# RWKV outputs in one run per group of four chunks, and half-array matmuls that alternate between two heads

## The chip, the cores and the metric

The kernel runs on one core of a Trainium2 chip. A core has a matrix engine (TensorE, PE in the profile) that multiplies a stationary operand, loaded beforehand, by a moving one and writes to PSUM, eight banks of accumulators; a vector engine (VectorE, DVE), a scalar engine (ScalarE, ACT), a general engine (GpSimd, POOL), and queues that start DMA transfers (SyncE, SP). The engines work side by side, each in its own order, and wait for each other through semaphores. The metric is the device time of one execution in microseconds (us), median of several runs; lower is better.

## The reference

One decoder layer over 2048 tokens of width 1024, in fp32: a mixer of two groups of heads, a cross-attention to 256 memory tokens, a SwiGLU feed-forward network, each with a norm ahead and a residual add. The change touches the mixer alone, and in it mainly the eight RWKV heads of width 64:

```python
def rwkv7_scan(r, w, k, v, a, b):
    def step(S, inp):
        r_t, w_t, k_t, v_t, a_t, b_t = inp
        sa = jnp.einsum('bhij,bhj->bhi', S, a_t)
        S = S * w_t[:, :, None, :] + sa[..., None] * b_t[:, :, None, :] + v_t[..., None] * k_t[:, :, None, :]
        return S, jnp.einsum('bhij,bhj->bhi', S, r_t)
```

Each head keeps a 64x64 state S that is updated at every token; the token's output is the new state times r. The outputs are then normalised per head, gated, and multiplied with the output weights together with the outputs of four mLSTM heads.

## The kernel before

The stages follow each other: a pass that transposes the normed input, the mixer, the output projection, attention, and the feed-forward network in two parts. `mixer` calls `mixer_pass` four times; a pass handles two RWKV heads and one mLSTM head for all tokens. Tokens go in super-groups of 256, eight to a pass; a super-group is four chunks of 64 tokens. The two RWKV heads of a pass lie in the two halves of the 128 partitions (`halves`: 0 to 63 and 64 to 127).

A pass takes two super-groups at a time:

- `prepare` (L295) projects k, r and v with f16 matmuls that use the whole array (three products of high and low parts, `mm3`, L52 to L55), derives the decays with the low-rank products `wps` (L317), and forms per chunk the operands of the scan. `AR` holds side by side a (64 columns) and r (64 columns), scaled by decays; `KB` the two kinds of keys. The products of `KB` and `AR` (`aps`, L379) are made per head on that head's 64 rows, four chunks of 128 columns to a PSUM bank; DVE masks them into `M`, `RA` and `AY` (L381, L382, L384), and ACT copies a part of `AR` into `RA` (L383). `KB` is transposed on PE (`kbps`, L390) and copied to `KBt` (L391).
- `solve` (L394) inverts the strict triangles `M` of the chunks: POOL does it for blocks of 32, with DMAs to bring them into rows, and PE joins the blocks with 32x32 matmuls (`pps`, L438, and `xps`, L443), first all of one head and then all of the other, with an ACT copy after each.
- `scan` (L446) walks through the four chunks one after another. For each chunk, three matmuls per head follow each other, with a copy between: `RA` times `VS` (L457, copy L459), `M` times that (L466, copy L469 into `VX`), `KBt` times `VX` (L471), from which DVE makes the next chunk's state (L475). `VS` holds the state in one half of its rows and v in the other. Then come the outputs y of the chunk: `AR`'s r part, on the head's 64 rows, times the state (L478), and `AY` times `VX` (L479) on all 128, into `yps`; after every second chunk DVE copies `yps` to `y` (L481). `tail` normalises and gates y later.
- the mLSTM head's work on the same tokens (`mlstm`) follows, again mostly full-array f16 matmuls.

The order in which instructions stand on each engine is not that of the source. A planner simulates the program on a model of the engines and places each instruction when its operands would be ready, with the source order as its priority. So PE's queue holds the scan's short steps with f16 matmuls of the projections between them. Tiles come from pools with a number of buffers; who writes a buffer again waits for its last reader. The pool `sl` (five buffers to a name) holds what a super-group hands from `prepare` to `scan`, `t1` has one buffer to a name. The PSUM pool `pax`, two banks, serves `wps`, `sps`, `bps`, `vps`, `aps` and `kbps` in turn; `psc` has one bank for `ch`, the scan's steps, and one for `yps`.

Of the kernel before, what the change touches and what calls it, by code (L numbers as in the profile page):

```python
# [165 lines left out]
def pre_pass(c, I, T, pool):  # L166
    """u^T = normed x, the RWKV low-rank activations and the mLSTM gate rows, for all tokens."""
# [77 lines left out]
def mixer_pass(c, I, hp, tp, T):  # L245
    """The RWKV heads 2*hp and 2*hp + 1 and the mLSTM head hp; leaves y^T in DRAM."""
# [48 lines left out]
    def prepare(sg, u, M):  # L295
# [6 lines left out]
        g.AR = sl.tile([P, 4, P], F32, tag="AR", name="AR")  # L302
        g.RA = sl.tile([P, 4, 2, 64], F32, tag="RA", name="RA")
# [47 lines left out]
        nc.vector.scalar_tensor_tensor(g.AR[:, :, 0:64], sq.rearrange(v4, n=4), c.kk[:, 0, ct:ct + 1], E[:, :, 0:64],  # L351
# [9 lines left out]
        nc.vector.tensor_tensor(g.AR[:, :, 64:128], r.rearrange(v4, n=4), E[:, :, 1:65], ALU.mult)  # L361
# [10 lines left out]
        for h in range(2):  # L372
            nc.gpsimd.tensor_copy(g.VX[halves[1 - h], :, h], g.VS[halves[1 - h], :, h])
        for h in range(2):
            b, ob = halves[h], halves[1 - h]
            kc = slice(64 * (1 - h), 64 * (1 - h) + P)
            aps = tp.pax.tile([P, 4, P], F32, tag="ax", name="aps")
            for n in range(4):
                nc.tensor.matmul(aps[:, n], lhsT=KB[b, n, kc], rhs=g.AR[b, n], start=True, stop=True)  # L379
            bc = lambda r, cc: c.mask[r, cc].unsqueeze(1).to_broadcast([r.stop - r.start, 4, 64])  # L380
            nc.vector.tensor_tensor(g.M[b], aps[b, :, 0:64], bc(b, b0), ALU.mult)  # L381
            nc.vector.tensor_tensor(g.RA[ob, :, h], aps[ob, :, 0:64], bc(ob, b0), ALU.mult)  # L382
            nc.scalar.copy(g.RA[b, :, h], g.AR[b, :, 0:64])  # L383
            nc.vector.tensor_tensor(g.AY[:, :, h], aps[:, :, 64:128], bc(slice(0, P), b1), ALU.mult)  # L384
        for h in range(2):
            b = halves[h]
            kc = slice(64 * (1 - h), 64 * (1 - h) + P)
            kps = tp.pax.tile([P, 4, 64], F32, tag="ax", name="kbps")
            for n in range(4):
                nc.tensor.transpose(kps[:, n], KB[b, n, kc], c.ident[b, b])  # L390
            nc.scalar.copy(g.KBt[:, :, h], kps)  # L391
        return g

    def solve(MX, NG):  # L394
        """Turns each chunk's strict triangle M into the transposed inverse of I - M^T, in place."""
# [39 lines left out]
        lohi = [(slice(64 * h, 64 * h + 32), slice(64 * h + 32, 64 * h + 64)) for h in range(2)]  # L435
        for a, b in lohi:
            for i in range(NU):
                nc.tensor.matmul(pps[b, i], lhsT=MXu[a, i, 32:64], rhs=T1[a, i], start=True, stop=True)  # L438
            nc.scalar.copy(T1[b].rearrange("p n (c e) -> p n e c", e=2), pps[b].rearrange("p n (e c) -> p n e c", e=2))
        xps = tp.psx.tile([P, NU, 32], F32, tag="sx", name="xps")  # L440
        for a, b in lohi:
            for i in range(NU):
                nc.tensor.matmul(xps[a, i], lhsT=T1[b, i], rhs=MXu[b, i, 32:64], start=True, stop=True)  # L443
            nc.scalar.copy(MXu[a, :, 32:64], xps[a])

    def scan(sg, g, g2, fresh):  # L446
# [4 lines left out]
        for n in range(4):  # L451
            ch = tp.psc.tile([P, 3, 64], F32, tag="ch", name="ch")
            if n % 2 == 0:
                yps = tp.psc.tile([P, 2, 64], F32, tag="Y", name="yps")
            to = halves[n % 2]
            for h in range(2):
                nc.tensor.matmul(ch[halves[h], 0], lhsT=g.RA[:, n, h], rhs=g.VS[:, n, h], start=True, stop=True)  # L457
# [12 lines left out]
            for h in range(2):  # L470
                nc.tensor.matmul(ch[halves[h], 2], lhsT=g.KBt[:, n, h], rhs=g.VX[:, n, h], start=True, stop=True)  # L471
# [4 lines left out]
            for h in range(2):  # L476
                b = halves[h]
                nc.tensor.matmul(yps[to, h], lhsT=g.AR[b, n, 64:128], rhs=g.VS[b, n, h], start=True, stop=False)  # L478
                nc.tensor.matmul(yps[to, h], lhsT=g.AY[:, n, h], rhs=g.VX[:, n, h], start=False, stop=True)  # L479
            if n % 2 == 1:  # L480
                nc.vector.tensor_copy(y[:, n // 2], yps)  # L481
# [168 lines left out]
def mixer(c, I, T):  # L650
    tc = c.tc
    with ExitStack() as ctx:
        tp = Ctx()
        for name, bufs, space in (("x", 2, None), ("w", 10, None), ("u", 8, None), ("t2", 1, None),
                                  ("t1", 1, None), ("m2", 2, None), ("k", 2, None), ("sl", 5, None), ("s2", 2, None), ("MX", 3, None), ("pmm", 2, PSUM),
                                  ("pax", 2, PSUM), ("psc", 1, PSUM), ("psx", 1, PSUM), ("pml", 1, PSUM)):
            kw = {"space": space} if space is not None else {"side": "right"} if name == "sl" else {}
            setattr(tp, name, ctx.enter_context(tc.tile_pool(name=f"x{name}", bufs=bufs, reuse_waits="tile", **kw)))
        for hp in range(4):
# [750 lines left out]
```

## Time and profile before

| | |
|---|---|
| median of 3 runs | 3165.73 us (3163.65 to 3174.46) |
| span of the profiled execution | 3167.2 us |
| PE, DVE, ACT, POOL busy | 97%, 68%, 41%, 38% of the span |
| mixer, about 104 to 1480 us: PE busy | 1334.8 of 1376 us |
| records of L478 and L479, the outputs | 512 each |
| records of L379 (aps), L390 (kbps) | 512, 256 |
| records of L438 (pps), L443 (xps) | 512 each |

The profile is of one execution, and the span is that execution's own time. A group of instructions is given by its line in the kernel, engine, operation, the tiles written and read, the rows x columns of the array that a matmul uses, and the number of records; an fp32 matmul leaves two records, an f16 matmul or an fp32 transpose one. In the order of time, a row gives start and length in us, and instructions of one kind that stand together are merged with their number. The length of a matmul is modelled; its start is measured.

### The profile page before, as it was taken

The page shows a single profiled execution, that of the slowest core. Times are in us where ns is not written, and L with a number is a line of the kernel's source. Part 1 is how long each engine was busy: PE and PEld are TensorE (multiplying, and loading weights), DVE is VectorE, ACT ScalarE, POOL GpSimd, SP SyncE. Part 2 cuts the span into 40 slices and gives each one's busy share as a digit, 9 for nine tenths or more (in the row PEclk, how much of TensorE's full clock was granted, in tenths as well). Part 3 has the DMA queues.
Part 4 walks back from the last instruction along what each step waited for, and adds up shares of the span by engine and source line. Part 5 has one row for each costly group of instructions (what it writes and reads, how often), then busy time and mean ns, then how long its engine had stood idle before and what let it go on. Part 6 is the DMA issues. An engine that isn't in the chain of part 4 may idle for free. (4 is left out here: it accounts for less than half of the span.)

```text
span 3167.2 us, 55759 instructions
## 1 busy us (share of the span) xinstructions
PE 3065.2 (97%) x20515; PEld 1855.3 (59%) x20515; DVE 2162.1 (68%) x4182; ACT 1290.2 (41%) x3098; POOL 1190.6 (38%) x2179
## 2 busy tenths in 40 slices
PE   7899999999999999999999999999999999899998
PEld 4688777777777767755645554444444444344444
DVE  6567877676767757744878888555554444897975
ACT  6444544454445434522756664222222222423432
POOL 2165545454545446201511124222222221553642
PEclk9899999899999989899999999999999999999999
DMA  8522422232213222554423337212112111454442
GB/s 271 128 75 60 106 61 74 60 96 61 72 47 81 71 72 67 162 167 154 144 84 120 115 129 281 81 54 67 56 58 74 54 53 54 165 188 157 133 145 83
DMA packets 393966, 331.01 MB, mean 105 GB/s; under 512 B 92654, under 2 KB 343772, under 8 KB 392796
## 3 DMA queue, kind: packets, MB, share of 16 engines
q1 hardware_dynamic: 393692, 327.45, 34.3%
q8 instruction: 161, 2.64, 0.4%
q14 instruction: 113, 0.93, 0.1%
HBM read 231.86 MB, written 95.49 MB: 103 GB/s over the span
## 5 line engine op out<-in xcount | busy, mean ns | idle before, releaser
L53 PE MATMUL pp<-u,wb 128*128 128x512 f16 x1232 | 468.1, 380 | 12.3 <-DVE e L1115 8.4
L54 PE MATMUL pp<-u,wb 128*128 128x512 f16 x1232 | 467.9, 380 | 0.0
L55 PE MATMUL pp<-u,wb 128*128 128x512 f16 x1232 | 467.6, 380 | 0.0
L1115 DVE TENSOR_TENSOR e<-pp,e 128x512 f32<-128x512 f32 x308 | 208.5, 689 | 300.3 <-PE pp L55 287.5
L55 PE MATMUL dps<-w,gS 128*128 128x512 f16 x616 | 234.1, 380 | 9.2 <-DVE gS L49 9.2
L54 PE MATMUL dps<-w,gS 128*128 128x512 f16 x616 | 234.2, 380 | 1.7 <-DVE w L49 1.7
L53 PE MATMUL dps<-w,gS 128*128 128x512 f16 x616 | 234.0, 380 | 0.0
L420 POOL TENSOR_TENSOR X<-X,tmp 64x126 f32<-64x126 f32 (+22 forms) x496 | 203.6, 410 | 31.0
L54 PEld LDWEIGHTS <-wb 128*128 128x128 f16 x1232 | 120.8, 98 | 155.6 <-issue 11.8
L418 POOL TENSOR_TENSOR tmp<-M,X 64x126 f32<-64x126 f32 (+22 forms) x496 | 187.0, 377 | 61.6 <-DMA M<-md 34.4
L53 PEld LDWEIGHTS <-wb 128*128 128x128 f16 x1232 | 120.8, 98 | 150.1 <-DMA u<-u_d 4.3
L55 PEld LDWEIGHTS <-wb 128*128 128x128 f16 x1232 | 120.8, 98 | 146.3 <-issue 1.3
L1131 POOL TENSOR_TENSOR S<-raw 128x512 f32<-128x512 f32 x22 | 33.8, 1536 | 405.0 <-DVE wb L49 405.0
L53 PEld LDWEIGHTS <-wh 128*128 128x128 f16 x1280 | 128.9, 101 | 27.0 <-issue 2.5
L53 PE MATMUL qps<-uh,wh 128*128 128x256 f16 x512 | 144.3, 282 | 0.0
L54 PE MATMUL qps<-ul,wh 128*128 128x256 f16 x512 | 144.0, 281 | 0.0
L54 PEld LDWEIGHTS <-wh 128*128 128x128 f16 x1280 | 129.0, 101 | 25.4 <-issue 4.2
L55 PE MATMUL qps<-uh,wl 128*128 128x256 f16 x512 | 143.7, 281 | 0.0
L55 PEld LDWEIGHTS <-wl 128*128 128x128 f16 x1280 | 129.2, 101 | 22.9 <-issue 1.7
L53 PE MATMUL vops<-wh,uh 128*128 128x256 f16 x512 | 139.8, 273 | 0.8 <-ACT cv L533 0.6
L55 PE MATMUL vops<-wh,ul 128*128 128x256 f16 x512 | 139.8, 273 | 0.0
L54 PE MATMUL vops<-wl,uh 128*128 128x256 f16 x512 | 139.8, 273 | 0.0
(430 smaller groups left out, 8104.8 us busy)
## 6 DMA issues: line engine op xcount, KB each, us to landing
g_d<-e SPq DMA_DIRECT2D x88, 256.0 KB
uh<-u_d SPq DMA_DIRECT2D x144, 128.0 KB
ul<-u_d SPq DMA_DIRECT2D x144, 128.0 KB
h<-h_d SPq DMA_DIRECT2D x32, 512.0 KB
acc<-h_d SPq DMA_DIRECT2D x32, 512.0 KB
u_d<-ub SPq DMA_DIRECT2D x56, 256.0 KB
ga<-g_d SPq DMA_DIRECT2D x32, 384.0 KB
raw<-in_ffn_w_gate_dram SPq DMA_DIRECT2D x22, 512.0 KB
```

Source lines behind the costliest of these rows:

```text
L53: nc.tensor.matmul(out, lhsT=lhs[0], rhs=rhs[0], start=start, stop=False)
L54: nc.tensor.matmul(out, lhsT=lhs[0], rhs=rhs[1], start=False, stop=False)
L55: nc.tensor.matmul(out, lhsT=lhs[1], rhs=rhs[0], start=False, stop=stop)
L418: nc.gpsimd.tensor_tensor(tv, M[:, s, s + 1:32].unsqueeze(2).to_broadcast(shp), X[:, s, 0:ncl].unsqueeze(1).to_broadcast(shp), ALU.mult)
L420: nc.gpsimd.tensor_tensor(X[:, s + 1:32, 0:ncl], X[:, s + 1:32, 0:ncl], tv, ALU.add)
L1115: add = lambda o, x, y: nc.vector.tensor_tensor(o, x, y, ALU.add)
L1131: nc.gpsimd.tensor_tensor(s[0], a[1][0], a[1][1], ALU.add)
```

## The change

Outputs: `AR` becomes a tile with one buffer, and a new tile `RR` of five buffers, [128, 4 chunks, 2 heads, 128], takes the place of `RA`. Its first 64 columns are what `RA` held. Its last 64 hold r on the head's own rows, copied by ACT together with the other part, and zeros on the other head's rows, which POOL writes once ahead of the passes. So the product with r now runs over all 128 rows, where the v part of `VS` meets the zeros. The outputs of all four chunks are made after the scan's last matmul of the super-group (`issue_after` sets their place on PE behind it), in a `yps` of four times 64 columns, and DVE copies it once.

Alternation: the matmuls of `wps`, `aps`, `kbps`, `pps` and `xps`, which use a part of the array's rows, no longer do all of one head and then the other, but one of each in turn. For `wps`, `aps` and `kbps` both heads' banks are taken ahead. The copies after `pps` and `xps` follow when both heads are done. The diff also takes docstrings out.

```diff
-        g.AR = sl.tile([P, 4, P], F32, tag="AR", name="AR")
-        g.RA = sl.tile([P, 4, 2, 64], F32, tag="RA", name="RA")
+        AR = tp.t1.tile([P, 4, P], F32, tag="AR", name="AR")
+        g.RR = next(tp.RR)
...
-        wps = []
-        for q in range(2):
-            b = halves[q]
-            wps.append(tp.pax.tile([P, SGN], F32, tag="ax", name="wps"))
-            mm3(nc, wps[q], (c.lwa[0][b, cs], c.lwa[1][b, cs]), (xwa[0][b], xwa[1][b]), True, True)
+        wps = [tp.pax.tile([P, SGN], F32, tag="ax", name="wps") for _ in range(2)]
+        for x, y in ((0, 0), (0, 1), (1, 0)):
+            for q in range(2):
+                b = halves[q]
+                nc.tensor.matmul(wps[q], lhsT=c.lwa[x][b, cs], rhs=xwa[y][b], start=x + y == 0, stop=x == 1)
...
+        kcs = [slice(64 * (1 - h), 64 * (1 - h) + P) for h in range(2)]
+        axs = [tp.pax.tile([P, 4, P], F32, tag="ax", name="aps") for _ in range(2)]
+        for n in range(4):
+            for h in range(2):
+                b = halves[h]
+                nc.tensor.matmul(axs[h][:, n], lhsT=KB[b, n, kcs[h]], rhs=AR[b, n], start=True, stop=True)
         for h in range(2):
-            b, ob = halves[h], halves[1 - h]
-            kc = slice(64 * (1 - h), 64 * (1 - h) + P)
-            aps = tp.pax.tile([P, 4, P], F32, tag="ax", name="aps")
-            for n in range(4):
-                nc.tensor.matmul(aps[:, n], lhsT=KB[b, n, kc], rhs=g.AR[b, n], start=True, stop=True)
+            b, ob, aps = halves[h], halves[1 - h], axs[h]
...
-            nc.vector.tensor_tensor(g.RA[ob, :, h], aps[ob, :, 0:64], bc(ob, b0), ALU.mult)
-            nc.scalar.copy(g.RA[b, :, h], g.AR[b, :, 0:64])
+            nc.vector.tensor_tensor(g.RR[ob, :, h, 0:64], aps[ob, :, 0:64], bc(ob, b0), ALU.mult)
+            nc.scalar.copy(g.RR[b, :, h], AR[b])
...
+        kps = [tp.pax.tile([P, 4, 64], F32, tag="ax", name="kbps") for _ in range(2)]
+        for n in range(4):
+            for h in range(2):
+                b = halves[h]
+                nc.tensor.transpose(kps[h][:, n], KB[b, n, kcs[h]], c.ident[b, b])
         for h in range(2):
-            b = halves[h]
-            kc = slice(64 * (1 - h), 64 * (1 - h) + P)
-            kps = tp.pax.tile([P, 4, 64], F32, tag="ax", name="kbps")
-            for n in range(4):
-                nc.tensor.transpose(kps[:, n], KB[b, n, kc], c.ident[b, b])
-            nc.scalar.copy(g.KBt[:, :, h], kps)
+            nc.scalar.copy(g.KBt[:, :, h], kps[h])
...
+        for i in range(NU):
+            for a, b in lohi:
+                nc.tensor.matmul(pps[b, i], lhsT=MXu[a, i, 32:64], rhs=T1[a, i], start=True, stop=True)
         for a, b in lohi:
-            for i in range(NU):
-                nc.tensor.matmul(pps[b, i], lhsT=MXu[a, i, 32:64], rhs=T1[a, i], start=True, stop=True)
             nc.scalar.copy(T1[b].rearrange("p n (c e) -> p n e c", e=2), pps[b].rearrange("p n (e c) -> p n e c", e=2))
...
-            for h in range(2):
-                b = halves[h]
-                nc.tensor.matmul(yps[to, h], lhsT=g.AR[b, n, 64:128], rhs=g.VS[b, n, h], start=True, stop=False)
-                nc.tensor.matmul(yps[to, h], lhsT=g.AY[:, n, h], rhs=g.VX[:, n, h], start=False, stop=True)
-            if n % 2 == 1:
-                nc.vector.tensor_copy(y[:, n // 2], yps)
+        yps = tp.psc.tile([P, 2, 2, 64], F32, tag="Y", name="yps")
+        with tc.issue_after(last.ins):
+            for m in range(2):
+                for h in range(2):
+                    for n in (2 * m, 2 * m + 1):
+                        nc.tensor.matmul(yps[halves[n % 2], m, h], lhsT=g.RR[:, n, h, 64:128], rhs=g.VS[:, n, h],
+                                         start=True, stop=False)
+                    for n in (2 * m, 2 * m + 1):
+                        nc.tensor.matmul(yps[halves[n % 2], m, h], lhsT=g.AY[:, n, h], rhs=g.VX[:, n, h],
+                                         start=False, stop=True)
+        nc.vector.tensor_copy(y, yps)
...
+        rr = [tp.RR.tile([P, 4, 2, P], F32, name=f"RR{i}") for i in range(5)]
+        for t in rr:
+            tc.nc.gpsimd.memset(t[64:128, :, 0, 64:128], 0.0)
+            tc.nc.gpsimd.memset(t[0:64, :, 1, 64:128], 0.0)
+        tp.RR = cycle(rr)
```

More of the change, by code (lines that the diff above doesn't have):

```diff
@@ L350, in prepare @@
         nc.vector.tensor_tensor(sq, sq, k, ALU.mult)
-        nc.vector.scalar_tensor_tensor(g.AR[:, :, 0:64], sq.rearrange(v4, n=4), c.kk[:, 0, ct:ct + 1], E[:, :, 0:64],
+        nc.vector.scalar_tensor_tensor(AR[:, :, 0:64], sq.rearrange(v4, n=4), c.kk[:, 0, ct:ct + 1], E[:, :, 0:64],
                                        op0=ALU.mult, op1=ALU.mult)
@@ L360, in prepare @@
         nc.scalar.copy(KB[:, :, 128:192], KB[:, :, 0:64])
-        nc.vector.tensor_tensor(g.AR[:, :, 64:128], r.rearrange(v4, n=4), E[:, :, 1:65], ALU.mult)
+        nc.vector.tensor_tensor(AR[:, :, 64:128], r.rearrange(v4, n=4), E[:, :, 1:65], ALU.mult)
         nc.vector.scalar_tensor_tensor(ta, r, col(c, R_RK + ct), ta, op0=ALU.mult, op1=ALU.mult)
@@ L435, in solve @@
         lohi = [(slice(64 * h, 64 * h + 32), slice(64 * h + 32, 64 * h + 64)) for h in range(2)]
+        for i in range(NU):
+            for a, b in lohi:
+                nc.tensor.matmul(pps[b, i], lhsT=MXu[a, i, 32:64], rhs=T1[a, i], start=True, stop=True)
         for a, b in lohi:
-            for i in range(NU):
-                nc.tensor.matmul(pps[b, i], lhsT=MXu[a, i, 32:64], rhs=T1[a, i], start=True, stop=True)
             nc.scalar.copy(T1[b].rearrange("p n (c e) -> p n e c", e=2), pps[b].rearrange("p n (e c) -> p n e c", e=2))
         xps = tp.psx.tile([P, NU, 32], F32, tag="sx", name="xps")
+        for i in range(NU):
+            for a, b in lohi:
+                nc.tensor.matmul(xps[a, i], lhsT=T1[b, i], rhs=MXu[b, i, 32:64], start=True, stop=True)
         for a, b in lohi:
-            for i in range(NU):
-                nc.tensor.matmul(xps[a, i], lhsT=T1[b, i], rhs=MXu[b, i, 32:64], start=True, stop=True)
             nc.scalar.copy(MXu[a, :, 32:64], xps[a])
@@ L452, in scan @@
             ch = tp.psc.tile([P, 3, 64], F32, tag="ch", name="ch")
-            if n % 2 == 0:
-                yps = tp.psc.tile([P, 2, 64], F32, tag="Y", name="yps")
-            to = halves[n % 2]
             for h in range(2):
-                nc.tensor.matmul(ch[halves[h], 0], lhsT=g.RA[:, n, h], rhs=g.VS[:, n, h], start=True, stop=True)
+                nc.tensor.matmul(ch[halves[h], 0], lhsT=g.RR[:, n, h, 0:64], rhs=g.VS[:, n, h], start=True, stop=True)
             R = tp.s2.tile([P, 64], F32, tag="R", name="R")
@@ L470, in scan @@
             for h in range(2):
-                nc.tensor.matmul(ch[halves[h], 2], lhsT=g.KBt[:, n, h], rhs=g.VX[:, n, h], start=True, stop=True)
+                last = nc.tensor.matmul(ch[halves[h], 2], lhsT=g.KBt[:, n, h], rhs=g.VX[:, n, h], start=True, stop=True)
             for h in range(2):
@@ L654, in mixer @@
         for name, bufs, space in (("x", 2, None), ("w", 10, None), ("u", 8, None), ("t2", 1, None),
-                                  ("t1", 1, None), ("m2", 2, None), ("k", 2, None), ("sl", 5, None), ("s2", 2, None), ("MX", 3, None), ("pmm", 2, PSUM),
+                                  ("t1", 1, None), ("m2", 2, None), ("k", 2, None), ("sl", 5, None), ("RR", 1, None), ("s2", 2, None), ("MX", 3, None), ("pmm", 2, PSUM),
                                   ("pax", 2, PSUM), ("psc", 1, PSUM), ("psx", 1, PSUM), ("pml", 1, PSUM)):
-            kw = {"space": space} if space is not None else {"side": "right"} if name == "sl" else {}
+            kw = {"space": space} if space is not None else {"side": "right"} if name in ("sl", "RR") else {}
             setattr(tp, name, ctx.enter_context(tc.tile_pool(name=f"x{name}", bufs=bufs, reuse_waits="tile", **kw)))
+        rr = [tp.RR.tile([P, 4, 2, P], F32, name=f"RR{i}") for i in range(5)]
[3 more added lines that the diff above has]
+        tp.RR = cycle(rr)
         for hp in range(4):
```

## Prediction

> **What bounds the kernel now.** I read the page's totals first, then the busy time of the two halves of the span, then what PE waited for in the first half, and last the order of time on PE around the matmuls that the change touches.
>
> ```profile
> span 3167.2 us, 55759 instructions
> PE 3065.2 (97%) x20515; PEld 1855.3 (59%) x20515; DVE 2162.1 (68%) x4182; ACT 1290.2 (41%) x3098; POOL 1190.6 (38%) x2179
> ```
> ```profile
> 104.00:1480.00 1376.00, 1334.81 (x11770) 1015.87 (x11768) 933.60 (x2414) 600.69 (x1824) 612.92 (x1654) 0.96 0.32 85
> 1480.00:3167.00 1687.00, 1649.72 (x8002) 789.06 (x8000) 1164.24 (x1630) 623.39 (x1152) 555.95 (x448) 1.00 0.34 110
> ```
> ```profile
> PE ch L457 <- DVE RA L382: 4.4, 1, 4.4
> ```
>
> All edits lie in the mixer, which runs from about 104 to 1480 us (columns of the second fence: stretch, its length, then busy us of PE, weight loads, DVE, ACT, POOL; then the granted clock). PE is busy for 1335 of 1376 us there, DVE for 934, ACT 601, POOL 613. The wait that costs PE most in this stretch (third fence: total us, times, longest) comes to 4.4 us, and its whole idle time to 41. So the order of PE's own instructions sets the pace, and a microsecond taken from PE's queue counts, unless other work then ends last. A busy PE is no proof of dense PE, because a record's end is modelled; the start times say more, and the rest is built on them.
>
> **The price of a change of array shape.** The timeline gives start, length, line, tiles, rows x columns of the array, and how many records were merged; an fp32 matmul leaves two records.
>
> ```profile
> 182.81 0.27 PE L54 MATMUL rps<-ul,wh 128*128 128x256 f16 x1
> 182.92 0.27 PE L55 MATMUL rps<-uh,wl 128*128 128x256 f16 x1
> 183.12 1.71 PE L379 MATMUL aps<-AR,KB 64*128 64x128 f32 x16
> 184.76 0.28 PE L53 MATMUL vps<-uh,wh 128*128 128x256 f16 x1
> ```
> Two full-array f16 matmuls start 0.11 us apart. The step from a full one to one on 64 rows is 0.20, so each such crossing costs some 0.09 us, and the way back costs too. That is the first thing that the change can save; the second is that two parts of the array can work at once:
>
> ```profile
> 609.45 0.27 PE L479 MATMUL yps<-VX,AY 128*64 128x64 f32 x1
> 609.45 0.27 PE L471 MATMUL ch<-VX,KBt 128*64 128x64 f32 x1
> 609.55 0.22 PE L479 MATMUL yps<-VX,AY 128*64 128x64 f32 x1
> 609.56 0.33 PE L471 MATMUL ch<-VX,KBt 128*64 128x64 f32 x3
> 609.82 0.33 PE L478 MATMUL yps<-VS,AR 64*64 64x64 f32 x2
> ```
> Matmuls that write different halves of the output partitions start within 0.01 us of each other.
>
> **The outputs (y).** 512 records of each kind, two to a matmul, are 128 chunks of two heads; and one chunk in order of time, in two places:
>
> ```profile
> L478 PE MATMUL yps<-VS,AR 64*64 64x64 f32 x512 | 85.0, 247 | 2.6 <-DVE VS L475 2.5
> L479 PE MATMUL yps<-VX,AY 128*64 128x64 f32 x512 | 83.3, 245 | 4.0 <-ACT VX L469 4.0
> ```
> ```profile
> 702.26 0.46 PE L390 MATMUL kbps<-ident,KB 64*128 64x64 f32 x4
> 702.65 0.32 PE L478 MATMUL yps<-VS,AR 64*64 64x64 f32 x2
> 702.91 0.34 PE L457 MATMUL ch<-VS,RA 128*64 128x64 f32 x4
> 703.17 0.46 PE L390 MATMUL kbps<-ident,KB 64*128 64x64 f32 x4
> ...
> 709.89 0.34 PE L471 MATMUL ch<-VX,KBt 128*64 128x64 f32 x4
> 710.06 0.28 PE L479 MATMUL yps<-VX,AY 128*64 128x64 f32 x2
> 710.27 0.33 PE L478 MATMUL yps<-VS,AR 64*64 64x64 f32 x2
> 710.52 0.33 PE L479 MATMUL yps<-VX,AY 128*64 128x64 f32 x2
> 710.78 0.28 PE L54 MATMUL vops<-wl,uh 128*128 128x256 f16 x1
> ```
> The early L478 takes 702.65 to 702.91, 0.26. Later, 709.89 to 710.78 is 0.89; four records of this shape with the way out take 0.26 (L457, 702.91 to 703.17), so the y part is 0.63. Together 0.89 a chunk, 128 of them: 114 us.
>
> What comes in its place is one run a group of four chunks: 16 matmuls, all 128 rows by 64 columns, alternating between the halves of the output. In the 609 us fence six records take 0.37 to the next shape, against 0.26 for four: a matmul more in the same half costs 0.11. Eight to each half, side by side: 0.9 a group when the run joins L471, which has the same shape, and 1.2 with its own way in and out. I take 1.05; 32 groups make 34 us. If the halves didn't overlap it would be 16 x 0.11 = 1.8, or 58. Net **-80** (bounds -56 and -85).
>
> **aps (L379).**
> ```profile
> 340.26 1.16 PE L379 MATMUL aps<-AR,KB 64*128 64x128 f32 x8
> 341.35 0.28 PE L53 MATMUL qps<-uh,wh 128*128 128x256 f16 x1
> ```
> One head alone costs 1.09 and the crossing into it 0.09: 1.18, two apart 2.36. Back to back, from 183.12 to 184.76 and a crossing, they cost 1.73, less than sixteen records one after another, so the second head's first records already run beside the first head's last. Alternating all the way should come near one head's time, 1.25. In the timeline five of 32 groups stand back to back, 27 apart: 27 x 1.1 + 5 x 0.5 = **-32** (with no more overlap than none, a crossing pair saved: -8).
>
> **wps, kbps, pps and xps.**
> ```profile
> 706.15 0.28 PE L53 MATMUL wps<-xwa,lwa 64*128 64x256 f16 x1
> ...
> 706.58 0.28 PE L53 MATMUL vops<-wh,uh 128*128 128x256 f16 x1
> ```
> ```profile
> 166.66 0.29 PE L53 MATMUL wps<-xwa,lwa 64*128 64x256 f16 x2
> ...
> 167.10 0.28 PE L53 MATMUL kps<-uh,wh 128*128 128x256 f16 x1
> ```
> ```profile
> 319.43 0.47 PE L390 MATMUL kbps<-ident,KB 64*128 64x64 f32 x8
> 319.84 0.28 PE L55 MATMUL vps<-uh,wl 128*128 128x256 f16 x1
> ```
> ```profile
> 542.79 0.69 PE L438 MATMUL pps<-T,MX 32*32 32x32 f32 x16
> 543.41 0.28 PE L53 MATMUL wps<-xwa,lwa 64*128 64x256 f16 x1
> ```
> The crossing in, 0.09, is added to each. wps: one head's three cost 0.43 + 0.09 = 0.52; where both heads' stand together already, six cost 0.44 + 0.09, about as much. Some 20 groups are apart: 20 x 0.5 = **-10** (-4 for the crossings alone). kbps: four cost 0.39 + 0.09 = 0.48 (702.26 above); eight together 0.41 + 0.09 = 0.50. About 24 groups are apart: 24 x 0.46 = **-11** (-5). pps and xps: sixteen records cost 0.62 + 0.09 = 0.71; 16 solves with two products of two heads. Alternating I expect 0.76 for both: 32 x 0.66 = **-21**; without overlap only the crossings, 0.2 each, -6.
>
> The Trainium skill (TensorE: Matmul & The Clock Gate, the section "Wait — 56ns, not 53.3ns?") says that starts of matmuls never lie closer than about 25 ns. The rows at 609.45 disagree for neighbouring halves; but if it held on the average for the 32x32 records, 32 of them would need 0.8 us, and pps and xps would give -13, the sum 8 less.
>
> **What is added, and its cover.**
> ```profile
> L379 PE MATMUL aps<-AR,KB 64*128 64x128 f32 x512 | 77.2, 297 | 7.1 <-DVE Sc L475 2.4 <-DVE VS L475 2.0 <-ACT RA L383 1.4
> L383 ACT COPY RA<-AR 64x256 f32<-64x256 f32 x64 | 25.7, 402 | 4.2 <-DVE AR L351 3.5
> L384 DVE TENSOR_TENSOR AY<-aps,mask 128x256 f32<-128x256 f32 x64 | 26.6, 416 | 0.5
> L373 POOL COPY VX<-VS 64x256 f32<-64x256 f32 x64 | 28.9, 451 | 53.3 <-ACT VS L371 40.0 <-PE yps L479 8.9 <-issue 1.8
> ```
> The ACT copy into RR is twice as wide, at most 0.40 us more in each of 64: 26 us on an engine that is idle for 775 of 1376, ahead of a solve that lies between it and its use; 0 taken, 13 if it were on the chain once a group. Ten memsets on POOL, by the nearest copy 0.45 each, 4.5 us once, while POOL has nothing to do (taken as 0). The y copies on DVE become half as many and twice as wide, slightly less. AR now has one buffer, so the next prepare's writes of it wait for the aps matmuls and the two copies; both come within a few us of the write and the next write a whole prepare later: 0. The run stands ahead of the next group's L457 and can hold it up by its 1.05 us; the y matmuls between chunks hold the chain up by 0.89 a chunk today: 0, and 34 at worst. The sum on PE is **-154**; with every lower bound it is -79.
>
> **How much of it reaches the end.** The half-speed clock is the other loss of this stage:
> ```profile
> 578.60:588.80 10.20, 9.55 (x51) 6.88 (x51) 5.36 (x16) 3.21 (x12) 2.99 (x8) 0.50 0.04 6
> ```
> The mean of 0.96 over the mixer's 1376 us is worth some 50 us, and PE's idle time 41. Both come where the f16 filler runs out and PE follows the scan's chain; there the y matmuls now stand in the gaps, and taking them out leaves a wait. DVE's share rises from 68 to 74%. I let these losses grow by 40, nearly by half: -154 + 40 = -114, and 3167.2 - 114 = 3053. The median of the runs lies 1.5 below the profiled execution: **3052 us**.
>
> **Rivals.** (1) The alternation brings no more overlap than there is, only fewer crossings: -79, with losses that grow by 20, half as much: 3107. Against it speak the wps and kbps fences, where the overlap is there.
> (2) The chain takes over: waits and half-speed stretches double, +90: 3102. For it: the 0.50 row above. Against: the scan's steps have f16 work beside them nearly everywhere. The Trainium skill (the same page, "HAM oscillation — how this bites in real kernels") ties the half-speed clock to idle gaps over some 3.4 us; the row at 578.60 has PE busy for 9.55 of 10.20 us at 0.50, so here it takes less. By the page no clock would be lost to short waits, only the waits would double: 3167 - 154 + 41, the forecast's own time.
> (3) The run doesn't stay together: the planner may set f16 matmuls between its pairs, since only its beginning is tied. A pair alone costs 0.26 + 0.09 = 0.35, eight 2.8 a group, 90 in all; y then saves 24, the sum is 98, and with the same 40 lost it is 3108.
> (4) **Slower.** Both banks of the pool that aps, kbps, wps, sps, bps and vps share are now claimed together. PE's queue is in order: kbps for both heads stands behind the masks of both, six DVE operations of 0.42 (2.5 us); aps stands behind four ACT copies out of vps, the next wps behind two KBt copies, none longer than L383's 0.40 (2.4 us). That is 4.9 us a group if none is covered; with 0.6 us lost to a clock that falls in such gaps, 5.5 x 32 = 176, and 3167 - 154 + 176 = 3189, 3188 as a median. It decides only from 4.8 us uncovered a group, 44 f16 steps that the planner would have failed to put there; today PE's idle time ahead of L379 is 7.1 us over all 32 groups, so it is unlikely.
>
> **Chances.** Forecast 0.62, (1) 0.12, (2) 0.12, (3) 0.06, (4) 0.08, a quarter of which near no change. A difference under 0.3% (9.5 us) is about what can't be told from no change. Faster 0.91, within 0.03, slower 0.06. The range goes from the whole sum and 15 us of regained clock, 2998, to beyond rivals 1 to 3, 3120; what is left out is (4) and a tail.
>
> **What would show it.** Right: L478 and L479 as one run of 32 records of 128*64 in about 1 us; L379 x16 in about 1.3; L390 x8, L438 x32 in about 0.8; a mixer that ends near 1365. Wrong: L379's sixteen records in 2 us (rival 1), clock below 0.93 or PE's waits over 90 us in the mixer (2), y in several pieces (3), long waits of kbps on AY or of aps on VS (4). The time after the mixer, 1687 us, should not move.

## The result, and the profile after

The changed kernel takes 3100.76 us (median of 4 runs, 3095.54 to 3102.05) against 3170.0 for the kernel before in the same runs (3163.65 to 3174.46). The ratio is 0.9782, with a 95% interval of 0.9765 to 0.9798: 69 us less, where 114 were forecast. One execution in the experiments, of `y_twice`, ran at a mean granted clock of 0.84 and took 3451.84 us; it is left out, and it is the only one of that kernel with a trace.

The page's totals, and the busy time of the two halves of the span (stretch, length, then PE, weight loads, DVE, ACT, POOL, then the granted clock), after the change:

```profile
span 3099.0 us, 55710 instructions
PE 2956.4 (95%) x20515; PEld 1776.2 (57%) x20515; DVE 2155.9 (70%) x4150; ACT 1299.8 (42%) x3098; POOL 1199.7 (39%) x2189
```
```profile
104.00:1410.00 1306.00, 1224.58 (x11772) 936.61 (x11771) 927.11 (x2379) 610.30 (x1824) 622.35 (x1669) 0.96 0.33 89
1410.00:3099.00 1689.00, 1649.77 (x7989) 787.82 (x7986) 1163.34 (x1630) 622.88 (x1151) 555.29 (x448) 1.00 0.33 110
```

The second row is that of before (1687 us, PE busy 1649.72). So the gain is in the mixer, which ends near 1410 instead of 1480, and not near 1365 as forecast. PE is busy for 110 us less there, and its idle time has doubled, from 41 to 81 us. What PE waits for in the mixer (total us, times, longest):

```profile
PE aps L379 <- ACT VS L371: 11.4, 5, 7.2
PE ch L472 <- ACT VX L470: 11.1, 21, 1.1
PE vps L53 <- DVE k L292: 10.9, 5, 5.3
PE ch L458 <- DVE VS L476: 9.3, 8, 2.3
PE ch L467 <- ACT R L460: 5.4, 14, 1.0
```

No single wait took the place of the work. In these rows the scan's three steps (L458, L467, L472) wait 26 us together, and the projections for DVE (`vps` behind `k`) 11.

The outputs came out as forecast: in all 32 groups one run of 32 records right behind L472, in 24 of them in about a microsecond. The order of time on PE, in a place where the next chunk's first step follows:

```profile
1115.33 0.34 PE L472 MATMUL ch<-VX,KBt 128*64 128x64 f32 x4 [0.53 <-ACT VX L470]
1115.49 0.29 PE L482 MATMUL yps<-VS,RR 128*64 128x64 f32 x4
1115.61 0.29 PE L485 MATMUL yps<-VX,AY 128*64 128x64 f32 x4
...
1116.31 0.29 PE L485 MATMUL yps<-VX,AY 128*64 128x64 f32 x4
1116.51 0.34 PE L458 MATMUL ch<-VS,RR 128*64 128x64 f32 x4
```

From 1115.49 to 1116.51 are 1.02 us for what cost 4 x 0.89 before. The 32x32 products come in one block of 32 records in 0.62 us, where a block of 16 took that before:

```profile
349.36 0.69 PE L440 MATMUL pps<-T,MX 32*32 32x32 f32 x32
349.98 0.28 PE L53 MATMUL vops<-wh,uh 128*128 128x256 f16 x1
```

`aps` shows both what alternation can do and that it mostly didn't take place:

```profile
158.80 1.16 PE L379 MATMUL aps<-AR,KB 64*128 64x128 f32 x16
159.89 0.49 PE L577 MATMUL ncp<-vx,Em 128*128 128x129 f32 x2
...
382.45 1.16 PE L379 MATMUL aps<-AR,KB 64*128 64x128 f32 x8
383.54 0.28 PE L53 MATMUL qps<-uh,wh 128*128 128x256 f16 x1
```

At 158.80 both heads' sixteen records take 1.09 us. At 382.45 one head's eight take the same 1.09. Only 6 blocks in the whole mixer have the form of the first row; 43 have that of the second.

**A ledger.** To compare kernels I put each start-to-start time on PE in the mixer to the first of the two records; what a step into a partial-array shape costs above 0.109 us is put to that shape, what exceeds 0.21 us (0.23 behind a full-array record) counts as waiting, and time at half speed counts half, the other half standing under "clock". In us:

| kernel | y | aps | kbps | wps | pps, xps | scan (ch) | waits | clock | median |
|---|---|---|---|---|---|---|---|---|---|
| before | 124 | 72 | 29 | 26 | 44 | 127 | 43 | 51 | 3170.0 |
| after | 33 | 68 | 25 | 26 | 24 | 132 | 82 | 58 | 3100.8 |
| change | -91 | -3 | -4 | 0 | -20 | +5 | +38 | +7 | -69 |

Work fell by 114 and losses rose by 45: 69 us, against 68.2 between the two spans.

### The profile page after: what moved, and what is told of

It reads as the page before. It is cut to its first block, busy times and chain, and to the rows that moved or that the text cites. A ratio compares the mean times of both kernels' runs of the same rounds, so it can differ in the third digit from the quotient of the medians.

```text
span 3099.0 us, 55710 instructions
## 1 busy us (share of the span) xinstructions
PE 2956.4 (95%) x20515; PEld 1776.2 (57%) x20515; DVE 2155.9 (70%) x4150; ACT 1299.8 (42%) x3098; POOL 1199.7 (39%) x2189
## 5 line engine op out<-in xcount | busy, mean ns | idle before, releaser
L420 POOL TENSOR_TENSOR tmp<-M,X 64x126 f32<-64x126 f32 (+22 forms) x496 | 194.9, 393 | 74.2 <-DMA M<-md 45.9
```

Source lines behind the costliest of these rows:

```text
L420: nc.gpsimd.tensor_tensor(tv, M[:, s, s + 1:32].unsqueeze(2).to_broadcast(shp), X[:, s, 0:ncl].unsqueeze(1).to_broadcast(shp), ALU.mult)
```

## The experiments

Where nothing else is said, an edit is one to the changed kernel. Each kernel ran together with the kernel before; a ratio is to that, with its 95% interval.

### Each part by itself

`y_only` keeps the outputs' run and puts the loops of wps, aps, kbps, pps and xps back to head after head. `solve_only` is the kernel before with the loops of pps and xps alone, `pax_only` the kernel before with those of wps, aps and kbps alone. The cores of the three:

```diff
-        axs = [tp.pax.tile([P, 4, P], F32, tag="ax", name="aps") for _ in range(2)]       # y_only, against the changed kernel
-        for n in range(4):
-            for h in range(2):
-                b = halves[h]
-                nc.tensor.matmul(axs[h][:, n], lhsT=KB[b, n, kcs[h]], rhs=AR[b, n], start=True, stop=True)
         for h in range(2):
...
+            aps = tp.pax.tile([P, 4, P], F32, tag="ax", name="aps")
+            for n in range(4):
+                nc.tensor.matmul(aps[:, n], lhsT=KB[b, n, kc], rhs=AR[b, n], start=True, stop=True)
...
+        for i in range(NU):                                  # solve_only, against the kernel before
+            for a, b in lohi:
+                nc.tensor.matmul(pps[b, i], lhsT=MXu[a, i, 32:64], rhs=T1[a, i], start=True, stop=True)
         for a, b in lohi:
-            for i in range(NU):
-                nc.tensor.matmul(pps[b, i], lhsT=MXu[a, i, 32:64], rhs=T1[a, i], start=True, stop=True)
...
+        axs = [tp.pax.tile([P, 4, P], F32, tag="ax", name="aps") for _ in range(2)]       # pax_only, against the kernel before
+        for n in range(4):
+            for h in range(2):
+                b = halves[h]
+                nc.tensor.matmul(axs[h][:, n], lhsT=KB[b, n, kcs[h]], rhs=g.AR[b, n], start=True, stop=True)
         for h in range(2):
...
-            aps = tp.pax.tile([P, 4, P], F32, tag="ax", name="aps")
-            for n in range(4):
-                nc.tensor.matmul(aps[:, n], lhsT=KB[b, n, kc], rhs=g.AR[b, n], start=True, stop=True)
```

> The outputs' run is kept, and wps, aps, kbps, pps and xps go head after head as before. Theory (the run takes some 86 us of PE work out, and about a third of it comes back as waits and half-speed clock where the f16 filler is short): about 50 us faster than before, L482 and L485 together about 33 us of PE time, PE's idle time in the mixer some 30 us up. Rival (the losses come from the two banks claimed together, not from the run): 75 us faster or more, idle time as before.

> Only pps and xps alternate; all else is the kernel before. Theory (PE's order sets the mixer's pace, so a short saving on it passes through): the 32x32 records fall from some 44 to 24 us of PE time, the time falls by 12 to 20 us. Rival (the solve's end is not on the path, since the scan's turn comes later): within 5 us of before.

> Only wps, aps and kbps alternate in the source; outputs and solve are the kernel before. Theory (the planner issues a head's matmuls as soon as that head's bank is free, and the other head's bank comes free later, so the alternation is mostly not carried out): still some 40 blocks of eight aps records, one head each, and a time within 10 us of before. Rival 1 (the alternation stands, and the array runs the heads side by side): some 35 to 50 us faster. Rival 2 (two banks claimed together hold PE up): 15 us slower or more.

Measured: `y_only` 3131.05 (ratio 0.9876, 0.9862 to 0.9890), `solve_only` 3153.59 (0.9956, 0.9943 to 0.9970), `pax_only` 3169.25 (0.9995, 0.9987 to 1.0004). By the ledger:

| kernel | y | aps | kbps | wps | pps, xps | scan | waits | clock |
|---|---|---|---|---|---|---|---|---|
| `y_only` | 33 | 73 | 25 | 25 | 45 | 132 | 71 | 65 |
| `solve_only` | 125 | 70 | 30 | 25 | 24 | 128 | 57 | 43 |
| `pax_only` | 126 | 69 | 29 | 26 | 45 | 127 | 45 | 53 |

By the ratios the run is worth 40 us, the 32x32 products 14 (10 to 18 by the interval), the three loops in the two banks nothing that can be measured: there the ledger's work on aps, kbps and wps is that of before within 3 us, and aps still stands in 42 blocks of eight records, for 47 before. The waits and the half-speed clock that eat nearly half of the run's saving come with the outputs' run (+28 and +14); `solve_only`'s work is 20 lower for 14 of time.

`y_solve` has the outputs' run and the 32x32 products, the three loops put back:

```diff
-        for n in range(4):
-            for h in range(2):
-                b = halves[h]
-                nc.tensor.transpose(kps[h][:, n], KB[b, n, kcs[h]], c.ident[b, b])
         for h in range(2):
...
+            kps = tp.pax.tile([P, 4, 64], F32, tag="ax", name="kbps")
+            for n in range(4):
+                nc.tensor.transpose(kps[:, n], KB[b, n, kc], c.ident[b, b])      # wps and aps likewise
```

> The changed kernel with wps, aps and kbps head after head in the source, as before the change. Theory (these three edits bring next to nothing here, because the planner mostly undoes them): within 8 us of the changed kernel. Rival (they bring the 15 us by which the changed kernel beats the sum of the single parts, 40 + 14 + 1): some 15 us slower than the changed kernel.

Measured 3111.99 (0.9822, 0.9809 to 0.9835): 56 less than before, the sum of 40 and 14 within what can be told. The whole change lies 11 us lower, though its three loops do nothing alone; in the ledger work differs by 5, waits by +13 and clock by -14. The intervals of the two ratios don't overlap, so the 11 us are real for these two programs. That lies between the two expectations, within 8 and some 15. Whether the loops earn them or another order on PE that falls out better, these runs don't tell.

### Forcing the alternation

`together` ties each matmul of wps, aps and kbps behind the one before it, and the first behind the last readers of both banks. So the planner can't separate the heads.

```diff
+        in_turn([lambda n=n, h=h, b=halves[h]: nc.tensor.matmul(
+            axs[h][:, n], lhsT=KB[b, n, kcs[h]], rhs=AR[b, n], start=True, stop=True)
+            for n in range(4) for h in (0, 1)], banks)   # banks: the op that reads bps (L365) and the VS copies
```

> The changed kernel, with wps, aps and kbps held to strict turns on PE and their first matmul held until both banks are free. Theory (the gain that was missed is real and only the order was lacking): aps as one block of sixteen records in about 1.3 us instead of two of 1.2, PE work some 35 to 40 us less than in the changed kernel, time 15 to 35 us under it, near 3075. Rival (waiting for both banks costs as much as the overlap brings): within 8 us of the changed kernel, or slower, with PE waiting for the copies out of vps and the masks.

Measured 3117.59 (0.9836, 0.9824 to 0.9849): 17 us more than after. It does what the change says: in 27 of 32 groups the sixteen records of aps stand together, in pairs of the two heads. The mixer over the same 1296 us, after and in `together`, and then what PE waits for in `together` (there L469, L478, L483 are the scan's three steps):

```profile
104.00:1400.00 1296.00, 1214.58 (x11707) 930.01 (x11706) 923.69 (x2373) 607.91 (x1819) 622.18 (x1668) 0.96 0.33 89
```
```profile
104.00:1400.00 1296.00, 1166.79 (x11604) 897.94 (x11604) 914.90 (x2367) 601.50 (x1814) 618.53 (x1667) 0.94 0.33 86
```
```profile
PE vps L53 <- DVE k L292: 19.7, 11, 7.1
PE ch L483 <- ACT VX L481: 17.9, 17, 3.3
PE ch L478 <- ACT R L471: 17.1, 19, 4.6
PE ch L469 <- DVE VS L487: 16.7, 20, 1.8
```

| kernel | y | aps | kbps | wps | pps, xps | scan | waits | clock | median |
|---|---|---|---|---|---|---|---|---|---|
| `together` | 33 | 40 | 16 | 19 | 23 | 133 | 116 | 84 | 3117.59 |
| `hold` | 33 | 56 | 18 | 18 | 23 | 135 | 95 | 77 | 3106.86 |

The work falls by another 44 us, to 158 below before, close to the 154 of the prediction's sum. But the scan's steps wait 52 us instead of 26, and waits and clock together grow by 60.

`hold` asks whether the waiting for both banks does that, or the order. It is the same kernel with the matmuls head after head:

```diff
-            for n in range(4) for h in (0, 1)], banks)
+            for h in (0, 1) for n in range(4)], banks)
```

> As the run with strict turns, with both banks awaited ahead of the first matmul, but head after head instead of alternating; so the holding is there and the overlap mostly is not. PE work lies some 20 us above that run's and 20 below the changed kernel's. Theory 1 (what made that run slower than the changed kernel is the holding of both banks, which leaves PE without a projection to do): 15 us or more slower than the changed kernel, about as slow as with strict turns or slower. Theory 2 (there PE only had too little to do for the clock, whatever the banks): with more work on PE than there, and less than in the changed kernel, a time between those two or under both.

Measured 3106.86 (0.9808, 0.9791 to 0.9825). `hold` has about 20 us more work than `together` and waits for both banks as that does; by the medians it is 11 us faster than `together` and 6 slower than after. So by the medians some 6 of `together`'s 17 us come with the wait for both banks and the rest with the order, though that has less work. The ratios' intervals overlap on both sides (with `together` by 0.0001), so this split is not shown. What the ledger shows is that each step of less work brings more of both losses: from after to `hold` work falls by 25 and waits and clock rise by 32, and from there to `together` work falls by 19 and they rise by 28.

### The run of the outputs

`y_two` makes two runs of eight matmuls, after the second and the fourth chunk. `y_twice` makes the whole run twice; the second overwrites the first with the same values. `three_banks` puts `yps` into the bank that the solve and the tail use, and gives the bank to the projections.

```diff
+            if n % 2 == 1:                  # y_two: inside the loop over the chunks, copied at once
+                m = n // 2
+                yps = tp.psc.tile([P, 2, 64], F32, tag="Y", name="yps")
...
-            for m in range(2):
+            for m in (0, 1, 0, 1):          # y_twice
...
-        yps = tp.psc.tile([P, 2, 2, 64], F32, tag="Y", name="yps")
+        yps = tp.psx.tile([P, 2, 2, 64], F32, tag="sx", name="yps")     # three_banks, and pmm 3 for 2
```

> The changed kernel with the outputs in a run of eight matmuls after every second chunk, instead of sixteen after every fourth. Theory 1 (a run at the group's end leaves the waits between the scan's steps without cover and holds up the next group): the same PE work, waits 10 to 20 us less, time 8 to 20 us under the changed kernel's. Theory 2 (the waits come from the work that is lacking beside the scan, wherever the outputs stand): within 8 us of the changed kernel.

> The changed kernel with the run of the outputs made twice over (the second overwrites the first with the same values): some 30 us more PE work, nothing else. Theory 1 (PE's own order still sets the pace): 25 to 30 us slower than the changed kernel. Theory 2 (after the change PE waits for others in good part of the mixer, so that work on it is partly free): 5 to 15 us slower.

> The changed kernel with the outputs' tile in the bank of the solve and the tails, and the freed bank given to the projections, which then have three. Theory (PE runs out of projections because their two banks wait for DVE to read them): PE's waits of projections for DVE L292, 11 us, fall to a few, and the time by 10 us or more. Rival (the waits are the scan's chain itself): within 8 us, or slower because the outputs wait for the bank they now share.

`y_two` took 3118.27 (0.9846, 0.9827 to 0.9864), 17 more than after; neither theory said so. Its outputs cost 36 us on PE (33 after) and its waits 82, as after; what differs is the clock loss, 89 for 58. The trace is of its slowest execution, 3125.77 us, so a part of the 31 is that one's own. Why the clock falls more often there isn't shown.

`y_twice` took 3127.98 (median of three; 0.9867, 0.9847 to 0.9887), 27 more than after, for a second run of 32 x 1.02 = 33 us of PE. What is added to PE there costs about 0.8 of its length, as its first theory had it.

`three_banks` took 3209.44 (1.0130, 1.0111 to 1.0149), slower than before, with waits of 108 and a clock loss of 126, for 82 and 58 after. Its longest waits of PE; the first is new, and the second was 9.3 after:

```profile
PE pps L440 <- DVE yc L513: 15.2, 10, 2.7
PE ch L458 <- DVE VS L476: 11.8, 15, 2.1
PE vps L368 <- DVE v L292: 11.1, 9, 3.7
```

The solve's products now wait until the tail of an earlier group has let go of their bank (`yc`, L513). With this edit the third bank for the projections brings less than the shared bank costs, and nothing can be said of its worth by itself.

### Other engines, and more work

`sw_act` moves one operation of each head and chunk from DVE to ACT, a scaling of the state that the scan's last step reads.

```diff
-                nc.vector.tensor_scalar(Sw[b], g.VS[b, n, h], g.W[b, n], None, op0=ALU.mult)
+                nc.scalar.activation(Sw[b], g.VS[b, n, h], AF.Copy, scale=g.W[b, n])
```

> The changed kernel with the scaled old state of each chunk (L464, 256 operations of 0.30 us, 76 us of DVE) made by ACT. Theory (DVE's queue, in its order, is what the scan's steps and the projections' banks wait for once PE has less to do): PE's waits for DVE (L292, L476) fall and the time by 10 to 25 us. Rival (the scan's own chain of steps, in which ACT has two copies a chunk, is what PE waits for): no gain or slower by up to 15 us, since ACT's queue is on that chain.

Measured 3100.77 (0.9785, 0.9768 to 0.9802), the time of after. Over the same stretch as above DVE is busy for 848 us instead of 924:

```profile
104.00:1400.00 1296.00, 1215.13 (x11682) 932.62 (x11680) 848.09 (x2115) 690.39 (x2072) 622.31 (x1673) 0.95 0.33 88
```

So taking 76 us from DVE's queue and putting 82 on ACT's is worth nothing here. PE's waits for DVE did not fall: `vps` waits 10.9 us behind `k` in both, and L458 9.9 for 9.3 behind `VS`; L467 waits 10.7 for 5.4 behind ACT's copy. So there is no sign that DVE's load is the bound, though a gain on DVE that an equal cost on ACT hides can't be ruled out by the time alone.

`f16_more` adds PE work instead: nine full-array f16 matmuls a group ahead of the first projection, into the same bank, where the projection then overwrites them.

```diff
+            if j == 0:
+                for k in range(3):
+                    h, l = wts[1][k]
+                    mm3(nc, ps, (h[:, 0:P], l[:, 0:P]), u[k], k == 0, k == 2)
```

> The changed kernel with nine full-array f16 matmuls more in every super-group, ahead of the mLSTM's q projection, whose first one overwrites what they leave: 288 x 0.109 = 31 us more work on PE, of the kind that stands between the scan's steps, and off the scan's chain. Theory 1 (PE's own order sets the pace): 25 to 31 us slower than the changed kernel, and then the 28 us of the doubled outputs were their PE time, not their place. Theory 2 (PE waits for the scan's chain in good part of the mixer, and spare f16 work fills these waits and keeps the clock up): less than 15 us slower; then the doubled outputs cost 28 because they stand on that chain.

Measured 3125.02 (0.9855, 0.9838 to 0.9871), 24 us more for 288 matmuls of 0.109 us, 31 us together. So PE's own order still sets the pace for work that is added, at about 0.8 of its length. Taken with `together`, the two directions differ: 31 us more cost 24, and 44 us less gained nothing, though `together` also has PE await both banks.

`em_first` concerns the longest single wait after the change, in the first group. All engines in order of time, after:

```profile
127.78 1.16 PE L379 MATMUL aps<-AR,KB 64*128 64x128 f32 x8
134.32 0.69 ACT L566 ACTIVATE Em<-mb,tk 128x128 f32<-128x128 f32 x2 [9.14 <-DMA mb<-m_d]
135.03 1.09 ACT L371 COPY VS<-vps 64x128 f32<-64x128 f32 x4
136.17 2.07 PE L379 MATMUL aps<-AR,KB 64*128 64x128 f32 x8 [7.24 <-ACT VS L371]
```

ACT's queue has the mLSTM's `Em` ahead of the copies out of `vps`, and `Em` waits 9.14 us for its first DMA; PE waits 7.24 for the bank behind it. `em_first` places these two operations behind the copies in the first group:

```diff
-            nc.scalar.activation(E[:, n], mb[:, ts], AF.Exp, bias=c.tk[:, 0, hp, ch:ch + 1], scale=-1.0)
+            with tc.issue_after(vs_last[3].ins) if hp == 0 and sg == 0 else nullcontext():
+                nc.scalar.activation(E[:, n], mb[:, ts], AF.Exp, bias=c.tk[:, 0, hp, ch:ch + 1], scale=-1.0)
```

> The changed kernel with one edit: in the very first super-group, ACT makes the mLSTM's decay tile Em, which waits for a late DMA, behind the copies out of vps instead of ahead of them. Theory (the 7.2 us in which PE waits there for the second head's bank is a loss of ACT's queue order, once): that wait goes and the time falls by 4 to 8 us. Rival (PE would wait for something else there): no gain.

Measured 3096.64 (3093.97 to 3100.46; ratio 0.9775, 0.9762 to 0.9788), with this left of the wait:

```profile
PE aps L381 <- ACT VS L373: 4.2, 4, 1.3
```

The wait of 7.2 us is gone; the longest of this kind is now 1.3. The medians lie 4 us apart and the intervals overlap. (The two traced spans, 3092.3 and 3099.0, differ by 6.7, but the spans of after alone lie 6.5 apart, from 3093.8 to 3100.3.) It is the fastest version measured, but not set apart from after by these runs.

### Why the heads stay apart: the other bank is held

The traces tell who holds the two banks of `pax` while aps is made. The group whose second head stands at 382.45 above, after:

```profile
371.24 0.70 PE L364 MATMUL bps<-ta,bones 128*128 128x256 f32 x2 [0.64 <-DVE ta L362]
373.41 1.08 ACT L371 COPY VS<-vps 64x128 f32<-64x128 f32 x4
377.75 1.13 PE L379 MATMUL aps<-AR,KB 64*128 64x128 f32 x8 [1.47 <-DVE AR L351]
381.80 0.42 DVE L386 TENSOR_TENSOR AY<-aps,mask 128x256 f32<-128x256 f32 x1
...
384.52 0.41 DVE L386 TENSOR_TENSOR AY<-aps,mask 128x256 f32<-128x256 f32 x1
384.85 0.41 DVE L512 TENSOR_TENSOR yc<-yc,bon 128x256 f32<-128x256 f32 x1
385.30 0.42 DVE L365 TENSOR_TENSOR bon<-bps,v 128x256 f32<-128x256 f32 x1
```

`bps` is written at 371.24. Its only reader is L365, which makes `bon`, and L365 comes at 385.30. All that time one bank is taken, 14.5 us here and 22 in the median of the groups 7 to 31. The bank of `vps` is free at 374.5, the first head uses it at 377.75, its last mask (L386) ends at 382.22, and 0.23 later the second head begins: it takes the same bank. No order of the loops can put two heads side by side into one bank.

L365 is late because `bon` has five buffers, and L512 is what reads the one it is to write, for the group five earlier. L365 starts 0.04 us after that L512 ends. In the trace of after L365 follows this L512 by 0.03 to 1.3 us in each of the groups 7 to 31 (of 0 to 31), and the second head's first record always comes after the first head's L386, by 0.15 to 2.8 us. Over the kernels, groups of 32 in which aps stands together (no gap of 0.5 us between its sixteen records), by whether L365 had ended by the start of aps (or within 0.5 us of it):

| kernel | L365 done: together / apart | L365 later: together / apart |
|---|---|---|
| before, after, `y_only` | 5 / 2 | 0 / 25 |
| `solve_only`, `pax_only`, `y_solve`, `y_two`, `sw_act`, `em_first` | 6 / 1 | 0 / 25 |
| `f16_more` | 4 / 3 | 0 / 25 |
| `three_banks` | 4 / 1 | 0 / 27 |
| `together` | 27 / 5 | none |
| `hold` | 26 / 6 | none |

That the bank is held until L365, and that L365 follows L512, is read from starts and ends, in every kernel alike. (In `together` and `hold` the edit itself puts aps behind L365, so their rows show only that the heads then stand together.) That another buffer for `bon` would bring the heads together wasn't tried.

## Why the prediction was right, and where it failed

**The outputs: right, and under-sized.** Forecast -80 with 1.05 us a run; the run takes 1.02 and the ledger has -91, of which the scan's steps give back 5, probably since they no longer share their way in and out with L478 and L479: -86. The old y part had cost 0.97 a chunk (124 / 128) where two places gave 0.89.

**pps and xps: right.** Forecast -21, measured -20.4. The row at 349.36 has 32 records in 0.62 us, 19 ns each. The Trainium skill (TensorE: Matmul & The Clock Gate, "Wait — 56ns, not 53.3ns?") has it that starts come no closer than about 25 ns, and with that the row disagrees. The prediction makes this rule worth -13; by its own terms, the estimate of 0.8 us from that rule and the crossing of 0.09 against twice 0.71, it would be 32 x 0.53 = -17.

**aps, kbps, wps: the step that failed.** "Alternating all the way should come near one head's time, 1.25" and hence -32, -11 and -10; measured -3, -4 and 0. The size of an alternating block was right (1.09 and the crossing), but the step took it that 27 separate groups would become alternating ones because the source says so. In 25 of 32 groups they can't, since the second bank isn't free. The trace of before shows that too, for whoever reads all engines beside the rows of PE from which the prediction priced one head. A group of before:

```profile
375.15 0.60 PE L364 MATMUL bps<-ta,bones 128*128 128x256 f32 x2
...
381.77 0.94 PE L379 MATMUL aps<-AR,KB 64*128 64x128 f32 x7
383.88 0.42 DVE L384 TENSOR_TENSOR AY<-aps,mask 128x256 f32<-128x256 f32 x1
386.11 1.16 PE L379 MATMUL aps<-AR,KB 64*128 64x128 f32 x8
...
389.63 0.41 DVE L365 TENSOR_TENSOR bon<-bps,v 128x256 f32<-128x256 f32 x1
```

Even the lower bounds (-8, -5, -4), which took it that crossings at least would be saved, were too high. 46 us of the forecast are missing here. The outputs saved 6 more than forecast and the losses took 5 more, so the whole miss is 45.

**Losses: near in size, by luck.** They were to grow by 40, and grew by 45 (waits 38, clock 7): the waits nearly doubled and the clock's loss hardly moved. But the 40 stood against a sum of 154, and the 45 came with 114. With the whole sum carried out, in `together`, the losses grow by 106 and the gain is 52: that is near rival 2, which had 90. So the forecast's -154 + 40 did not come about when the alternation was forced. The time measured, 3100.8, is 49 above the forecast; the stated range holds it because it was drawn to take in rivals 1 to 3.

**The rivals.** Rival 1 (3107) is near in time but not in cause: the array does overlap the heads where they alternate. Rival 2 (3102) is nearer still, but after has half of its growth of the losses (45 for 90) and a granted clock of 0.96, so its time is met with less work saved and less lost. Rival 3 didn't come: 25 of 32 runs of outputs stand alone behind L472, in the other 7 the next L458 follows at once, and none is broken up by f16 matmuls. Rival 4 has 11.4 us of waits of aps on VS, 7.2 of them once, in place of 176.

**What stays open.** PE's order sets the price of added work, and moving work off DVE brings nothing; yet work taken from aps, kbps and wps, in the one form in which it was taken, brings no time. A loop through the five buffers (tail, L365, the banks, solve, scan, tail) would do that, and the place of L365 in each group speaks for it; no run here changed it. The trace of after speaks against it in most groups: the solve's last product ends 3 to 23 us ahead of the scan that wants it in 12 of 16 pairs of groups. Only in the first pair of each pass does it end after that scan's first step, by 13 to 25 us in passes 2 to 4, and there the scan's second step comes 15 to 28 us behind the first instead of 0.6 to 5. The kernel before has these three gaps as well (16 to 27 us), and the change leaves them. From 142 to 1389 us the scans of the 32 groups follow each other in a row: each group's first step (L458) starts 1.0 to 5.9 us after the last L472 of the group before. What sets their length, 20 to 54 us where the solve is in time, PE's other work between the steps or the steps' own waits, is not separated here.

## What to carry to other kernels

Before you price an alternation between two buffers, look in the trace when each buffer's last reader ends; a bank held by an unhurried reader undoes any order of the loops. An operation that nothing waits for can still hold a bank that PE needs, so follow each buffer from its writer to its last reader. And where PE's filler has run out, price work that you take away by a run that forces it away: here 44 us less work, with both banks awaited, came with 60 us more of waits and half-speed clock.

## What the hardware showed that was not expected

**The clock falls without an idle gap.** Windows of 3.41 us, which is the grid on which the granted clock switches in the records (all stretches of the trace of after begin a whole number of 3.413 us apart; the columns are those of the first windows above, PE first, the clock behind POOL), after the change; and then the two windows of before ahead of the stretch that the prediction quotes:

```profile
568.08:571.49 3.41, 2.22 (x47) 2.03 (x45) 2.72 (x8) 2.51 (x8) 1.09 (x4) 1.00 0.00 0
571.49:574.90 3.41, 2.27 (x23) 1.65 (x21) 2.95 (x10) 0.94 (x4) 0.59 (x1) 1.00 0.13 19
574.90:578.32 3.42, 2.94 (x22) 2.10 (x22) 1.94 (x8) 1.55 (x6) 1.03 (x2) 0.50 0.25 60
578.32:581.73 3.41, 3.41 (x39) 1.75 (x38) 2.94 (x7) 2.34 (x9) 1.09 (x4) 0.50 0.35 99
581.73:585.14 3.41, 3.41 (x36) 2.25 (x31) 3.04 (x8) 1.99 (x6) 2.94 (x10) 0.50 0.23 63
585.14:588.55 3.41, 3.41 (x54) 2.68 (x52) 1.75 (x5) 1.34 (x4) 2.86 (x8) 1.00 0.02 5
```
```profile
571.80:575.20 3.40, 3.40 (x35) 2.64 (x33) 1.00 (x5) 1.10 (x4) 0.39 (x2) 1.00 0.13 39
575.20:578.60 3.40, 2.15 (x24) 1.36 (x23) 1.23 (x5) 0.79 (x4) 0.00 (x0) 1.00 0.14 39
```

The clock halves after one window with 23 or 24 records in it (571.49, and 575.20 of before), though PE counts as busy for two thirds of it and never idles longer than 0.53 us in the first of them. The window at 568.08 has no more busy time, 2.22 us, and the clock stays, so busy time doesn't decide; that window has 47 records. In these rows the clock comes back after a half-speed window that is busy throughout (581.73), but not after the first such window (578.32). An estimate for the whole mixer is the share of a window in which columns stream, at the pace of the f16 rows (256 columns in 0.109 us), the columns of an fp32 record counted twice. In the changed kernel the full-speed windows that were followed by another had a median share of 0.93; those ahead of a fall had 0.0 to 0.70, and in the kernel before 0.26 to 0.57. The two kinds overlap: 16 of 333 windows without a fall had 0.70 or less, down to 0.48, so a low share goes with the falls but doesn't settle when one comes. Where a scan step without filler brings a fall, it costs more than its wait: the half-speed stretch that follows lasts at least 3.4 us. There are 30 half-speed windows in the mixer of before, 34 after, 49 in `together`, 52 in `y_two`. The Trainium skill speaks of idle gaps over some 3.4 us (TensorE: Matmul & The Clock Gate, "HAM oscillation — how this bites in real kernels"); the window at 571.49, where the longest idle is 0.53 us, disagrees with that as a condition. The same page of the Trainium skill says in its next section, "A second HAM failure mode: psum-queue depth-cycling", that frequent short idles between groups of matmuls do it too, and the window at 571.49 agrees: 1.14 us idle in pieces of at most 0.53 us. So what the prediction draws "by the page" for rival 2 holds for the first of the two sections alone.

**Neighbouring tiles start 6 to 7 ns apart.** In the alternating blocks the starts come in pairs: 7 and 52 ns for the outputs' run (128x64, fp32), 7 and 105 for aps (64x128, fp32), 7 and 25 for the 32x32 products. So in these blocks the second half of the array is nearly free, once the two halves do alternate: sixteen aps records take the 1.09 us that eight take.
